# Layer border of a two-layer trunk: rows of x loaded in another place, sums and results tied differently, and the gate blocks of layer two run by token halves

## The chip, the cores and the metric

The kernel runs on one core of a Trainium2 chip. The core has a matrix engine (TensorE, PE in the profile), a vector engine (VectorE, DVE), a scalar engine (ScalarE, ACT), GpSimd (POOL) and SyncE (SP), whose queue issues most of the transfers. Each engine runs its instructions in the order in which they stand on it, and waits on semaphores for the others. The metric is the device time of one execution in microseconds, the median of several runs; less is better.

## The reference

Two layers of a hybrid trunk, on 512 tokens of width 2048, all in float32. Each layer normalises x, multiplies it by one wide input projection, runs two groups of heads on the columns, multiplies by an output projection, normalises again and adds the result to x:

```python
def hybrid_layer(x, w_in, w_out, g_pre, g_post, w_alpha, b_alpha, g_gla, g_att, rel_bias):
    h = rmsnorm(x, g_pre)
    z = h @ w_in
    gq, gk, gv, gg, ga, aq, ak, av, ag = split_columns(z)
    log_a = jax.nn.log_sigmoid(ga @ w_alpha + b_alpha) / GLA_TAU
    o_gla = rmsnorm(gla_chunk_causal(gq, gk, gv, log_a), g_gla) * jax.nn.silu(gg)
    o_att = rmsnorm(chunk_band_attention(aq, ak, av, rel_bias), g_att) * jax.nn.silu(ag)
    y = jnp.concatenate([o_gla, o_att], axis=-1) @ w_out
    return x + rmsnorm(y, g_post)

def reference(x, ...):
    h = x
    for l in range(DEPTH):          # DEPTH = 2
        h = hybrid_layer(h, ...)
    return h
```

(Shapes of heads are left out.) The border between the layers is what this document is about: the last output projection of layer one, `x + rmsnorm(y, g_post)`, the next layer's `rmsnorm(x, g_pre)`, and the next layer's first column blocks, the attention gate `ag`.

## The kernel before

**Weights.** Float32 products are made of three products of halves: each 1024-column piece of a weight block is split into a high part `wh` (cast on ACT, line 198) and a low part `wl` (difference on DVE, line 207), and each operand into a high and a low part in the same way (`split`: ACT line 105, DVE line 106). One weight *job* is 512 KB of weights: SP loads it into a ring (`raw`, five buffers, or `H`, four), ACT casts it (four buffers of `wh`), DVE makes the low part (three of `wl`), and PE runs twelve matmuls of 128x512 (line 387 in `fast_gemm`, 309 in `std_gemm`). `stream` is the list of all jobs of the program in the order of use, and `ahead` prepares loads, casts and low parts a few jobs ahead.

**A layer.** Two gate blocks AG0 and AG1 go through `std_gemm`, then six pairs of blocks through `fast_gemm`, which makes two block columns out of seven products P1 to P7 instead of eight, on sums and differences of the halves of weights and operands. Four jobs make one product. The output projection is two such pairs, W01 and W23; their products run P1, P2, P5, P6, P3, P7, P4. P7 subtracts two weight halves on DVE (line 194) and P4 adds two (line 192) before their casts. The operands of P5, P6, P3 and P7 come from DRAM (`sa<-oS`), one 512 KB load for each job; P4's lie in SBUF.

**The border.** The four token tiles are two halves. The products of W23 give results for one column block `j` and one token half `h` at a time, which are handed to `project`, which squares them for the norm (ACT line 1322) and multiplies by the gain (DVE lines 344 and 1326). When half 0 of the tokens is complete (after P3's result `(1, 0)`), `finish` runs for it: `finish_both` reduces the squares (DVE line 1365), takes the reciprocal root on GpSimd (`rsqrt`, line 429, a `pow`), and updates x, `z = y * r + z` (DVE line 1377), storing the result (GpSimd line 1380). `prep_half` squares the new rows (ACT line 442, reduce on DVE line 443), takes a second reciprocal root, scales the rows (DVE line 496), transposes them on PE (line 510), copies them out of PSUM with the gain (ACT line 521) and splits them into operands. When P4 is complete, the same runs for half 1, whose rows lie in narrower pieces (two of 1024 and four of 512). Its operands are read by the second half of the gate blocks, and the forget gate's weights are loaded behind it (`load_forget_gate`, lines 693 to 709).

The old x comes from DRAM row piece by row piece (`residual`, line 457), tied to certain jobs of W23.

**Order.** The source says little of when something runs. A scheduler puts the instructions of each engine into one order, by its own estimate of when each is ready and by the order of the source; `tc.issue_after(i)` only says that what follows must not stand ahead of `i`. In the source, work at the border is a list of generators (`tasks`), of which `pace` takes steps between the matmuls at a rate given for each product.

**Gate blocks of layer two.** AG0 runs for token half 0 (eight jobs), then again, with its weights loaded again, for half 1 (eight jobs); AG1 runs once for all four token tiles (eight jobs of 24 matmuls).

## Time and profile before

| | us |
|---|---|
| median of 3 runs (lowest, highest) | 1625.25 (1624.55, 1625.42) |
| profiled execution | 1624.26 |
| its span | 1622.5 |
| PE busy in the span | 1603.1 |
| DVE busy | 1263.3 |
| ACT busy | 909.8 |

The clock of PE was 0.998 of full in the profiled execution. W23's last products end near 809 us of the span, the gate blocks of layer two run from 810 to 913. In rows of the timeline the columns are start and duration in us, engine, line, operation, what it writes and reads, its shape, and in brackets the idle time of that engine just before it and what ended that; `xN` means N instructions drawn together. Tile names stand without their numbers: `sa` an operand from DRAM, `wh` and `wl` the parts of a weight block, `mm` and `ax` PSUM tiles, `g` any of the large slots in SBUF, `sm` small columns. The row of a window gives busy time of each engine in that stretch.

### The profile page before, as it was taken

The page shows a single profiled execution, that of the slowest core. Times are in us where ns is not written, and L with a number is a line of the kernel's source. Part 1 is how long each engine was busy: PE and PEld are TensorE (multiplying, and loading weights), DVE is VectorE, ACT ScalarE, POOL GpSimd, SP SyncE. Part 2 cuts the span into 40 slices and gives each one's busy share as a digit, 9 for nine tenths or more (in the row PEclk, how much of TensorE's full clock was granted, in tenths as well). Part 3 has the DMA queues.
Part 4 walks back from the last instruction along what each step waited for, and adds up shares of the span by engine and source line. Part 5 has one row for each costly group of instructions (what it writes and reads, how often), then busy time and mean ns, then how long its engine had stood idle before and what let it go on. Part 6 is the DMA issues. An engine that isn't in the chain of part 4 may idle for free.

```text
span 1622.5 us, 24443 instructions
## 1 busy us (share of the span) xinstructions
PE 1603.1 (99%) x8938; PEld 1372.6 (85%) x8938; DVE 1263.3 (78%) x1640; ACT 909.8 (56%) x1497; POOL 133.0 (8%) x192
## 2 busy tenths in 40 slices
PE   9999999999999999999999999999999999999997
PEld 7888999998888778878778889999988887788886
DVE  5977778678777868988987567686786778689887
ACT  7554445666554556655694444456575555466644
POOL 0120000000000010100222000000100000101001
PEclk9999999999999999999999999999999999999999
DMA  9797686785868768697879576867868687686887
GB/s 371 258 366 282 226 304 203 241 292 176 293 206 292 255 223 307 227 344 250 330 254 391 200 269 242 295 210 234 313 214 278 214 292 254 223 303 237 333 301 197
DMA packets 132777, 433.97 MB, mean 267 GB/s; under 512 B 14277, under 2 KB 27077, under 8 KB 132625
## 3 DMA queue, kind: packets, MB, share of 16 engines
q1 hardware_dynamic: 115920, 371.79, 65.9%
q0 software_dynamic: 16160, 59.53, 10.0%
q8 instruction: 71, 1.16, 0.3%
q10 hardware_dynamic: 576, 1.08, 0.2%
q14 instruction: 50, 0.40, 0.1%
HBM read 372.83 MB, written 61.62 MB: 268 GB/s over the span
## 4 chain that ended last, share of the span: by engine, by line
PE 93%; DVE 2%; DMA 2%; issue 1%; ACT 1%; POOL 0%; DVEq 0%; SPq 0%; ACTq 0%
PE mm L387 52%; PE mm L377 18%; PE mm L309 10%; PE ax L931 2%; PE ax L387 2%; PE ax L1117 1%; PE ax L914 1%; DVE wl L207 1%; PE ax L741 1%; DMA raw<-in_w_dram 1%; PE ax L1089 1%; PE ax L894 1%; PE ax L893 1%; PE ax L892 1%; DMA sa<-oS 1%
## 5 line engine op out<-in xcount | busy, mean ns | idle before, releaser
L387 PE MATMUL mm<-wh,sa 128*128 128x512 f32 x1600 | 517.8, 394 | 1.4 <-DMA sa<-oS 0.8
L207 DVE TENSOR_TENSOR wl<-H,wh 128x1024 fp32r<-128x1024 f32 x256 | 312.5, 1222 | 105.8 <-PE mm L387 33.6
L198 ACT CAST wh<-H 128x1024 fp32r<-128x1024 f32 x256 | 268.4, 1051 | 218.1 <-PE mm L387 92.6
L387 PEld LDWEIGHTS mm<-wh,sa 128*128 128x128 f32 x1600 | 299.5, 188 | 73.8 <-issue 9.7
L198 ACT CAST wh<-raw 128x1024 fp32r<-128x1024 f32 (+1 forms) x229 | 240.0, 1052 | 208.1 <-PE mm L387 96.6
L207 DVE TENSOR_TENSOR wl<-raw,wh 128x1024 fp32r<-128x1024 f32 (+1 forms) x229 | 278.0, 1218 | 63.9 <-PE mm L387 29.8
L387 PE MATMUL mm<-wl,sa 128*128 128x512 f32 x800 | 312.6, 391 | 0.0
L377 PE MATMUL mm<-sa,wh 128*128 128x256 f32 x1280 | 237.4, 285 | 0.0
L387 PE MATMUL mm<-wh,a 128*128 128x512 f32 x640 | 211.3, 394 | 1.5 <-ACT wh L198 1.5
L377 PEld LDWEIGHTS mm<-sa,wh 128*128 128x128 f32 x1280 | 200.2, 191 | 0.3
L377 PE MATMUL mm<-sa,wl 128*128 128x256 f32 x640 | 181.0, 283 | 0.2 <-DVE wl L207 0.2
L192 DVE TENSOR_TENSOR H<-H,raw 128x1024 f32<-128x1024 f32 x144 | 175.3, 1222 | 1.2
L387 PEld LDWEIGHTS mm<-wl,sa 128*128 128x128 f32 x800 | 150.3, 188 | 30.0 <-DVE wl L207 0.3
L387 PEld LDWEIGHTS mm<-wh,a 128*128 128x128 f32 x640 | 119.4, 188 | 26.7 <-ACT wh L198 1.9
L387 PE MATMUL mm<-wl,a 128*128 128x512 f32 x320 | 125.6, 393 | 0.0
L377 PEld LDWEIGHTS mm<-sa,wl 128*128 128x128 f32 x640 | 122.5, 191 | 0.4 <-DVE wl L207 0.4
L429 POOL TENSOR_TENSOR sm<-sm,mhalf 128x2 f32<-128x2 f32 (+2 forms) x40 | 57.3, 1433 | 761.2 <-DVE sm L941 457.0
L194 DVE TENSOR_TENSOR raw<-H,raw 128x1024 f32<-128x1024 f32 x60 | 73.4, 1224 | 49.9 <-DMA raw<-in_w_dram 49.5
L387 PE MATMUL mm<-wh,g 128*128 128x512 f32 x320 | 101.4, 390 | 0.6 <-ACT ev L339 0.6
L377 PE MATMUL mm<-a,wh 128*128 128x256 f32 x512 | 95.4, 285 | 0.0
L339 ACT COPY ev<-mm 128x512 f32<-128x512 f32 x104 | 60.8, 584 | 60.4 <-PE mm L387 44.0
L213 DVE TENSOR_TENSOR H<-H,raw 128x1024 f32<-128x1024 f32 x48 | 58.7, 1223 | 39.8 <-DMA raw<-in_w_dram 39.5
(246 smaller groups left out, 2313.5 us busy)
## 6 DMA issues: line engine op xcount, KB each, us to landing
raw<-in_w_dram SPq DMA_DIRECT2D x307, 512.0 KB, 5.1
sa<-S SPq DMA_DIRECT2D x184, 512.0 KB, 4.4
H<-in_w_dram SPq DMA_DIRECT2D x64, 512.0 KB, 5.4
sa<-A SPq DMA_DIRECT2D x48, 512.0 KB, 6.0
S<-g POOLq DMA_DIRECT2D x32, 512.0 KB, 9.0
sa<-oS SPq DMA_DIRECT2D x32, 512.0 KB, 4.8
oS<-g POOLq DMA_DIRECT2D x16, 512.0 KB, 4.5
oS<-sa POOLq DMA_DIRECT2D x16, 512.0 KB, 5.6
```

The costliest lines, as they stand in the source:

```text
L192: nc.vector.tensor_tensor(out=h, in0=h, in1=r, op=ALU.add)
L194: nc.vector.tensor_tensor(out=r, in0=h, in1=r, op=ALU.subtract)
L198: last_cast[0] = nc.scalar.copy(self.wh[:, z, :], src[:, z, :]).ins
L207: last_low[0] = nc.vector.tensor_tensor(out=self.wl[:, z, :], in0=self.src[:, z, :], in1=self.wh[:, z, :].bitcast(F32), op=ALU.subtract).ins
L213: nc.vector.tensor_tensor(out=h, in0=h, in1=self.src, op=ALU.add)
L309: nc.tensor.matmul(pss[o], a(part, kk, o) if callable(a) else a[:, part, t], rhs[:, kk, :], start=(i == 0 and kk == 0 and m == 0), stop=(i ...
L339: nc.scalar.copy(e, src[t])
L377: nc.tensor.matmul(dst, lhs[:, kk, f], a[:, part, tok], start=(fresh and kk == 0 and m == 0 and ft % 2 == 0), stop=(c == 3 and kk == 1 and ...
L387: last_mm[0] = nc.tensor.matmul(out_ps[t], a[:, part, tok], rhs[:, kk, :], start=(fresh and kk == 0 and m == 0), stop=(c == 3 and kk == 1 ...
L429: nc.gpsimd.tensor_tensor(out=out_r, in0=v, in1=mhalf[:, : v.shape[-1]], op=ALU.pow)
L741: nc.tensor.matmul(ps[0:96, half * 256 : (half + 1) * 256], wga[kt // 10][:, kt % 10, :], op[:, i, (kt % 2) * 256 : (kt % 2 + 1) * 256], s ...
L931: nc.tensor.matmul(o, self.pt[i][:, j * P : (j + 1) * P], av[hd // 4, j // 2][:, j % 2, (hd % 4) * P : (hd % 4 + 1) * P], start=(j == 0), ...
```

## The change

1. The rows of x for half 0 are loaded in W23's P1 and P2 behind jobs 2 and 3 of each instead of 0 and 1, those for half 1 in P5 and P6 instead of P6 and P7.
2. P4's weight sums of layer one's W23 are tied behind updates of x for half 0: the first behind the second update, the other three behind the fourth.
3. In W23 of layer one, the results of P7 (`(1, 1)`) are tied behind the last row scaling of half 0; the results `(1, 0)` and `(0, 0)`, of P3 and P2, lose their tie.
4. Of the four row scalings of half 0, the two of the first token tile run on ACT.
5. The gate blocks of layer two run AG0 and AG1 for half 0, then AG0 and AG1 for half 1: 32 jobs of twelve matmuls where there were sixteen of twelve and eight of 24. PE's matmuls are the same in number; eight more weight blocks are loaded, cast and split.

```diff
@@ Job.high
-                with tc.issue_after(lows[-2]) if self.b0 >= NB_IN else nullcontext():
+                with ExitStack() as ties:
+                    if self.b0 >= NB_IN:
+                        ties.enter_context(tc.issue_after(lows[-2]))
+                    if k == "P4" and self.l < L - 1 and self.b0 == W23[0]:
+                        ties.enter_context(tc.issue_after(half_adds[3 if self.c else 1]))
                     if k in ("P5", "P6") or (k == "P4" and self.b0 >= NB_IN):
                         nc.vector.tensor_tensor(out=h, in0=h, in1=r, op=ALU.add)
@@ stream
-            stream += [Job(l, "std", c, AG0) for c in CO]
-            stream += [Job(l, "std", c, AG0) for c in CO]
-            stream += [Job(l, "std", c, AG1) for c in CO]
+            stream += [Job(l, "std", c, b) for half in range(2) for b in (AG0, AG1) for c in CO]
@@ prep_half
-                last_row = nc.vector.tensor_scalar(
-                    out=xn[j][i], in0=z, scalar1=r[:, j : j + 1], scalar2=None, op0=ALU.mult
-                ).ins
+                if half == 0 and j == 0:
+                    nc.scalar.activation(xn[j][i], z, AF.Copy, scale=r[:, j : j + 1])
+                else:
+                    last_row = nc.vector.tensor_scalar(
+                        out=xn[j][i], in0=z, scalar1=r[:, j : j + 1], scalar2=None, op0=ALU.mult
+                    ).ins
@@ layer
-            std_gemm(l, AG0, (0, 1), CO, operand_in, gate_evac(0), rate=1.2)
-            tasks.append(token_sums(l))
-            tasks.append(forget_gate())
-            std_gemm(l, AG0, (2, 3), CO, operand_in, gate_evac(0), rate=0.8)
-            std_gemm(l, AG1, range(NT), CO, operand_in, gate_evac(1), rate=1.3, lag=2)
+            for half in range(2):
+                for q, b in enumerate((AG0, AG1)):
+                    std_gemm(
+                        l, b, (2 * half, 2 * half + 1), CO, operand_in, gate_evac(q), rate=1.3, lag=2 * half * q,
+                    )
+                if half == 0:
+                    tasks.append(token_sums(l))
+                    tasks.append(forget_gate())
@@ finish_both
-                        nc.vector.scalar_tensor_tensor(
-                            out=z, in0=yt, scalar=r[:, j : j + 1], in1=z, op0=ALU.mult, op1=ALU.add
+                        half_adds.append(
+                            nc.vector.scalar_tensor_tensor(
+                                out=z, in0=yt, scalar=r[:, j : j + 1], in1=z, op0=ALU.mult, op1=ALU.add
+                            ).ins
                         )
@@ out_consume
-                with nullcontext() if n and (j, h) == (0, 1) else tc.issue_after(last_low[0]):
+                if n and not last:
+                    behind = half_rows[0] if (j, h) == (1, 1) else None
+                else:
+                    behind = None if n and (j, h) == (0, 1) else last_low[0]
+                with tc.issue_after(behind) if behind else nullcontext():
                     project(o, n + j, src, gains[j] if n else None, comb, begin if ending else None)
@@ residual
-            elif k in ("P6", "P7") or (k in ("P1", "P2") and c < 2):
-                half = int(k in ("P6", "P7"))
+            elif k in ("P5", "P6") or (k in ("P1", "P2") and c >= 2):
+                half = int(k in ("P5", "P6"))
```

The lines of the changed kernel stand a few numbers further down: 207 is 211, 198 is 202, 192 is 196, 1326 is 1334, 1365 is 1373, 1377 is 1386, 443 is 445, 496 is 501 on DVE and 499 on ACT.

What that does to the order on DVE where P7 turns into P4, from the second reduce of half 0's squares on. Before, the low parts of P4's first three jobs (`wl<-H`) stand between and right behind the updates of x (L1377, written to `g_1405` to `g_1408`):

```order
L1365 TENSOR_REDUCE sm_7751<-ssy_6933 128x1
L207 TENSOR_TENSOR wl_7805<-H_7189,wh_7775 128x1024
L192 TENSOR_TENSOR H_7277<-H_7277,raw_7810 128x1024
L1377 SCALAR_TENSOR_TENSOR g_1405_7311<-a_1326_6929,sm_7752,g_1405_7311 128x1024
L1377 SCALAR_TENSOR_TENSOR g_1406_7312<-g_1439_7473,sm_7752,g_1406_7312 128x1024
L1377 SCALAR_TENSOR_TENSOR g_1407_7313<-a_1329_6935,sm_7752,g_1407_7313 128x1024
L1377 SCALAR_TENSOR_TENSOR g_1408_7314<-g_1442_7479,sm_7752,g_1408_7314 128x1024
L207 TENSOR_TENSOR wl_7841<-H_7241,wh_7808 128x1024
L192 TENSOR_TENSOR H_7335<-H_7335,raw_7846 128x1024
L207 TENSOR_TENSOR wl_7892<-H_7277,wh_7844 128x1024
L443 TENSOR_REDUCE sm_7784<-sm_7786 128x1
```

Now the same stretch reads:

```order
L1373 TENSOR_REDUCE sm_7753<-ssy_6933 128x1
L1386 SCALAR_TENSOR_TENSOR g_1421_7395<-a_1326_6929,sm_7754,g_1421_7395 128x1024
L1386 SCALAR_TENSOR_TENSOR g_1422_7396<-g_1439_7472,sm_7754,g_1422_7396 128x1024
L196 TENSOR_TENSOR H_7189<-H_7189,raw_7741 128x1024
L1386 SCALAR_TENSOR_TENSOR g_1423_7397<-a_1329_6935,sm_7754,g_1423_7397 128x1024
L1386 SCALAR_TENSOR_TENSOR g_1424_7398<-g_1442_7478,sm_7754,g_1424_7398 128x1024
L196 TENSOR_TENSOR H_7241<-H_7241,raw_7779 128x1024
L445 TENSOR_REDUCE sm_7785<-sm_7787 128x1
L211 TENSOR_TENSOR wl_7806<-H_7189,wh_7777 128x1024
L196 TENSOR_TENSOR H_7277<-H_7277,raw_7811 128x1024
L445 TENSOR_REDUCE sm_7785<-sm_7813 128x1
L211 TENSOR_TENSOR wl_7841<-H_7241,wh_7809 128x1024
```

The updates moved ahead of P4's first weight sum and low part, and directly behind the reduce.

On DVE during the first AG0 pass, from the second reduce of half 1's squares on (`wl_8065` is the low part of the fourth job, `wl_8087` of the fifth, `a_15...` are operands of half 0, `g_1457`, `sg` and `bias` the rows of half 1). Before:

```order
L1365 TENSOR_REDUCE sm_8054<-ssy_7201 128x1
L207 TENSOR_TENSOR wl_8065<-raw_8019,wh_8035 128x1024
L1377 SCALAR_TENSOR_TENSOR g_1457_7548<-g_1377_7197,sm_8055,g_1457_7548 128x1024
L1377 SCALAR_TENSOR_TENSOR g_1458_7549<-g_1538_7903,sm_8055,g_1458_7549 128x1024
L207 TENSOR_TENSOR wl_8087<-raw_8037,wh_8067 128x1024
L106 TENSOR_TENSOR a_1548_7933<-H_7930,a_1548_7933 128x512
L1377 SCALAR_TENSOR_TENSOR sg_7550<-g_1380_7203,sm_8055,sg_7550 128x512
L1377 SCALAR_TENSOR_TENSOR sg_7551<-g_1380_7203,sm_8055,sg_7551 128x512
L106 TENSOR_TENSOR a_1550_7943<-H_7930,a_1550_7943 128x512
```

Now:

```order
L211 TENSOR_TENSOR wl_8065<-raw_8019,wh_8035 128x1024
L1334 TENSOR_TENSOR g_1541_7909<-mm_7292,t_1396_7285 128x512
L1373 TENSOR_REDUCE sm_8054<-ssy_7201 128x1
L106 TENSOR_TENSOR a_1548_7933<-H_7930,a_1548_7933 128x512
L106 TENSOR_TENSOR a_1550_7943<-H_7930,a_1550_7943 128x512
L106 TENSOR_TENSOR a_1556_7972<-H_7969,a_1556_7972 128x512
L1386 SCALAR_TENSOR_TENSOR g_1449_7506<-g_1377_7197,sm_8055,g_1449_7506 128x1024
L1386 SCALAR_TENSOR_TENSOR g_1450_7507<-g_1538_7903,sm_8055,g_1450_7507 128x1024
L1386 SCALAR_TENSOR_TENSOR sg_7508<-g_1380_7203,sm_8055,sg_7508 128x512
L1386 SCALAR_TENSOR_TENSOR sg_7509<-g_1380_7203,sm_8055,sg_7509 128x512
L1386 SCALAR_TENSOR_TENSOR bias_7510<-g_1541_7909,sm_8055,bias_7510 128x512
L1386 SCALAR_TENSOR_TENSOR bias_7511<-g_1541_7909,sm_8055,bias_7511 128x512
```

Here the fifth job's low part, which stood behind two updates, stands right behind all six.

On ACT behind P4's casts, `g_1518` and `g_1519` being the scaled rows of the first token tile, `H_7853` the first operand out of PSUM. Now:

```order
L202 CAST wh_7844<-H_7277 128x1024
L499 ACTIVATE g_1518_7821<-g_1421_7395,sm_7786 128x1024
L499 ACTIVATE g_1519_7823<-g_1422_7396,sm_7786 128x1024
L202 CAST wh_7895<-H_7330 128x1024
L202 CAST wh_7960<-raw_7897 128x1024
L1330 ACTIVATE t_1540_7906,ssy_7195<-t_1539_7904 128x512
L202 CAST wh_7999<-raw_7962 128x1024
L526 ACTIVATE H_7853<-ax_7848,gcol 128x256 x2
```

Before, the two L499 were not on this engine.

More of the change, by code (lines that the diff above doesn't have):

```diff
@@ L482, in hybrid_trunk @@
     full = {}
-    half_lows, half_turns, half_rows = [], [], [None]
+    half_adds, half_lows, half_turns, half_rows = [], [], [], [None]
     def prep_half(l, half, xs):
```

## The prediction

> **What bounds the kernel now.** I read the page's first and fourth parts, then the idle rows of TensorE (PE) in the timeline around the layer border, then the engines that end those waits.
>
> ```profile
> PE 1603.1 (99%) x8938; PEld 1372.6 (85%) x8938; DVE 1263.3 (78%) x1640; ACT 909.8 (56%) x1497; POOL 133.0 (8%) x192
> PE 93%; DVE 2%; DMA 2%; issue 1%; ACT 1%; POOL 0%; DVEq 0%; SPq 0%; ACTq 0%
> ```
>
> PE is the bound: 1603.1 of a 1622.5 us span, and both kernels give it the same matmuls. Only bubbles can move. Those within reach of the change:
>
> ```profile
> 771.00 0.84 PE L387 MATMUL mm<-wh,sa 128*128 128x512 f32 x3
> 771.68 0.39 PE L387 MATMUL mm<-wl,sa 128*128 128x512 f32 x1
> ...
> 785.98 0.39 PE L387 MATMUL mm<-wh,sa 128*128 128x512 f32 x1
> 786.61 0.47 PE L387 MATMUL mm<-wh,sa 128*128 128x512 f32 x1 [0.23 <-DMA sa<-oS]
> ...
> 789.22 0.39 PE L387 MATMUL mm<-wh,sa 128*128 128x512 f32 x1
> 790.18 0.47 PE L387 MATMUL mm<-wh,sa 128*128 128x512 f32 x1 [0.58 <-DMA sa<-oS]
> ...
> 792.80 0.39 PE L387 MATMUL mm<-wh,sa 128*128 128x512 f32 x1
> 793.83 0.50 PE L387 MATMUL mm<-wh,g 128*128 128x512 f32 x1 [0.64 <-ACT ev L339]
> ...
> 801.92 0.39 PE L387 MATMUL mm<-wh,g 128*128 128x512 f32 x1
> 803.60 0.33 PE L510 MATMUL ax<-cst,g 128*128 128x128 f32 x1 [1.29 <-DVE g L496]
> ...
> 822.16 0.61 PE L309 MATMUL mm<-wl,a 128*128 128x512 f32 x2
> ...
> 824.20 0.84 PE L309 MATMUL mm<-wh,a 128*128 128x512 f32 x3
> 825.19 0.50 PE L309 MATMUL mm<-wl,a 128*128 128x512 f32 x1
> 835.58 0.33 PE L510 MATMUL ax<-cst,g 128*128 128x128 f32 x1 [0.61 <-ACT g L521]
> 838.61 0.33 PE L510 MATMUL ax<-cst,g 128*128 128x128 f32 x1 [0.92 <-ACT g L521]
> 839.46 0.50 PE L309 MATMUL mm<-wh,g 128*128 128x512 f32 x1 [0.19 <-ACT g L105]
> ```
>
> Matmuls of 512 columns start 0.227 us apart (771.00, three of them, 771.68), so a weight block's twelve take 2.72 us. Start to start against that pace, the gaps cost more than the bracket shows: 786.61 costs 0.40, 790.18 costs 0.73 (both P7, waiting for operands), 793.83 costs 0.80 (P7 to P4), the half-0 transposes 1.45 and about 0.5, 825.19 costs 0.31 (three starts from 824.20 would be 824.88), the half-1 transposes up to 839.46 about 2.6 (with two small waits between). That is some 7 us, 0.43% of the time: the most the change can give.
>
> **The change part by part.** An operation on VectorE (DVE) or ScalarE (ACT) overlaps the next by some 0.08 us, so its pace is its duration less that: the first two starts below (784.93, 786.07) are 1.14 apart at 1.22 each.
>
> ```profile
> 779.22 1.22 DVE L194 TENSOR_TENSOR raw<-H,raw 128x1024 f32<-128x1024 f32 x1
> 784.93 1.22 DVE L207 TENSOR_TENSOR wl<-raw,wh 128x1024 fp32r<-128x1024 f32 x1
> 786.07 1.22 DVE L192 TENSOR_TENSOR H<-H,raw 128x1024 f32<-128x1024 f32 x1
> ...
> 787.80 0.15 DVE L1365 TENSOR_REDUCE sm<-ssy 128x1 f32<-128x5 f32 x1
> ...
> 792.04 1.28 DVE L1377 SCALAR_TENSOR_TENSOR g<-g,sm,g 128x1024 f32<-128x1024 f32 x1
> ...
> 802.79 2.74 DVE L496 TENSOR_SCALAR g<-g,sm 128x1024 f32<-128x1024 f32 x4 [0.61 <-POOL sm L429]
> ...
> 820.06 1.41 DVE L1377 SCALAR_TENSOR_TENSOR sg<-g,sm,sg 128x512 f32<-128x512 f32 x2
> ```
>
> Columns: start, duration, engine, line, operation. So: a low part (wl) or a weight sum 1.14, a reduce 0.06, a residual update 1.20 (half width 0.66), a row scaling 0.66; a half-width product 0.60 (row 801.49 further down).
>
> *Rows of x.* Six half-1 loads and the fourth half-0 load leave P7's stretch, where DMA stood at 408 GB/s (row 780 to 800 below). P7 then needs one operand and one weight block, 1.05 MB per 2.72 us, 385 GB/s: I take its two waits, 1.13 us, as gone, and P7's end at 791.9. In P5/P6 a job now brings an operand and at most a row, again 385 GB/s, with operands issued four jobs ahead: I take nothing. Bounds: 0 and the same 1.13 back.
>
> *P4's sums and P7's results.* DVE now goes: reduce, four updates with two of P4's sums among them, and only then P4's low parts. From 780.36 (779.22 + 1.14): half-width 0.60, wl 1.14, half-width twice, the first reduce, P7's last wl 1.14, half-width, the second reduce: 4 x 0.60 + 2 x 1.14 + 0.12 + 0.1 (duration of the last) = 785.25. Then the rsqrt on GpSimd:
>
> ```profile
> 540.48 0.71 POOL L429 TENSOR_TENSOR sm<-sm,mhalf 128x2 f32<-128x2 f32 x1 [41.00 <-DVE sm L433]
> 788.11 2.69 POOL L429 TENSOR_TENSOR sm<-sm,mhalf 128x2 f32<-128x2 f32 x1 [2.92 <-DVE sm L1365]
> 799.93 2.82 POOL L429 TENSOR_TENSOR sm<-sm,mhalf 128x2 f32<-128x2 f32 x1 [3.39 <-DVE sm L443]
> 801.49 0.69 DVE L344 TENSOR_TENSOR t<-ev,ev 128x512 f32<-128x512 f32 x1
> ```
>
> The same 128x2 op takes 0.71 us with DVE idle and 2.7 to 2.8 when DVE runs two-input operations back to back: the one at 799.93 ends 0.57 after DVE's last (801.49 + 0.69). In the new order DVE has nothing between the second reduce and the update, so I take 0.71, with 0.25 from reduce to rsqrt (787.80 + 0.15 to 788.11, and the hand-over): first update at 786.24. With 2.69 it is 788.2; that end goes into the range. [...]
>
> Then 2 x 1.20 + 1.14 + 2 x 1.20 + 1.14 + 0.06 (reduce) + 1.14 (wl of P4's first job) + 1.14 + 0.06 = 9.5: second reduce done at 795.7. P4's first wl is ready at 794.6, where PE wants it 0.45 after 791.9: a new wait of about 2.25 us in P4's first job. So what the three removed waits gave (1.13 + 0.80) is spent here. Behind that wl nothing else of P4 is late: its second job's wl is done at 796.9. The second rsqrt has two DVE operations behind it and ends 0.57 after them, so row scaling starts at 798.7 (before: 802.79). The transposes then wait about 0.2 instead of 2; the gate starts near 809.3.
>
> *Row scaling on ACT.* Two scalings leave DVE (1.3 us), two come to ACT, about 0.96 each. There they stand ahead of everything that makes the gate's operands:
>
> ```profile
> 805.50 2.30 ACT L521 ACTIVATE H<-ax,gcol 128x256 f32<-128x256 f32 x6 [1.45 <-PE ax L510]
> ...
> 812.48 0.66 ACT L1322 ACTIVATE t<-mm 128x512 bf16<-128x512 f32 x1
> ...
> 815.91 1.17 ACT L198 CAST wh<-raw 128x1024 fp32r<-128x1024 f32 x1
> 816.85 1.79 ACT L105 CAST a<-H 128x512 fp32r<-128x512 f32 x3
> ```
>
> Pace: L521 0.36, L105 0.52, L1322 0.60 with its accumulator read, a cast 0.95 (815.91 to 816.85). From 798.7 ACT runs without a pause: 2 scalings, 5 casts, 16 of L521, 4 of L105 and one like it, 4 squares of L1322: 1.9 + 4.8 + 5.8 + 2.6 + 2.4 = 17.5, so the last square that half 1's residual needs is done at 816.2 (before: 812.48 + 0.66 = 813.1). DVE then: low part, product, reduce, three operand low parts (L106, 0.60 each) and, 0.57 after these, the third rsqrt: half 1's first update at 819.9 (before 815.93).
>
> *Half 1's updates.* All six now stand in one piece ahead of the low part of AG0's fifth block: 2 x 1.20 + 4 x 0.66 = 5.0, then 1.14: wl at 826.1. PE reaches that wl at 809.3 + 4 x 2.72 + 0.45 = 820.7 and waits 5.4 us. Before, it passed the same matmul at 822.16.
>
> *Gate blocks by halves.* Half 1's transposes now have two AG1 jobs between them and 16 us until their operands are read, so no operand of half 1 is late if its rows are in time. After the wl at 826.1 DVE has an operand's low part, three wl, two reduces, six small low parts of the forget gate's weights (the row below), the fourth rsqrt (0.6 behind the last of these) and six scalings: 0.6 + 3.4 + 0.1 + 1.4 + 0.6 + at most 4.0 = 836.2, against PE's need at 826.1 + 2.3 + 3 x 2.72 + 0.45 = 837.0. The 2.6 us at 835 to 839 go, and the 0.3 at 825. Price: eight more blocks, each 512 KB of DMA, a cast (0.95) and a low part (1.14): 7.6 us on ACT and 9.1 on DVE, covered by the idle time in the windows below (columns: window, length, busy PE, PEld, DVE, ACT, POOL, clock, DMA share, GB/s).
>
> ```profile
> L106 DVE TENSOR_TENSOR g<-t,g 128x160 fp32r<-128x160 f32 (+1 forms) x6 | 1.4, 288 | 2.6 <-ACT g L105 2.6
> ```
>
> ```profile
> 780.00:800.00 20.00, 18.55 (x80) 14.33 (x79) 19.04 (x24) 12.88 (x21) 5.22 (x10) 1.00 1.03 408
> ...
> 865.00:888.00 23.00, 23.00 (x117) 19.46 (x116) 14.26 (x19) 10.09 (x15) 6.41 (x12) 1.00 1.03 408
> ...
> 900.00:913.00 13.00, 13.00 (x59) 10.78 (x58) 4.10 (x4) 4.02 (x6) 1.66 (x3) 1.00 0.55 197
> ```
>
> DVE is busy 14.26 of 23 us from 865 and 4.10 of the last 13, ACT less, so I cost these at nothing; without that room it would be the 9.1 us of DVE. DMA has none until 900: 4.2 MB more at 408 GB/s is 10 us of transfers, which find room after 900, if PE's lead of weights lasts that long. I take 0; the other end is the first rival. On SP's queue the load of the forget gate's w_ga now follows AG1's first block; that block's buffer is free when the fourth AG0 block's low part is done (817), and a load takes 4 to 5 us, so it is there before the 827 at which ACT wants it. GpSimd's stores of the updated rows go out with the updates, 0.54 us each, and nothing of the chain is queued behind them but the next rsqrt, which comes later anyway.
>
> **Sum.** PE passes the marked matmul 826.1 - 822.2 = 3.9 us (4.0 with the restart) later; the waits after it that go are 2.9. Net +1.1 us: profiled 1624.26 becomes 1625.4; the median of the runs shown is 1.0 above the profiled run, so 1626.4. Own range: -1 (second rsqrt not held up, 2 us) to +3.2 (first rsqrt 2.69, or P5/P6 paying the 1.13).
>
> **Rivals.** *Slower: weight loads starve in the second half of the gate.* Blocks are used every 2.72 us (193 GB/s) where AG1's took 5.44. Five raw buffers and 2.1 us of cast and low part hold that pace only while a load lands within 5 x 2.72 - 2.1 = 11.5 us.
>
> ```profile
> raw<-in_w_dram SPq DMA_DIRECT2D x4, 512.0 KB, 7.0
> ...
> q1 hardware_dynamic: 1382, 1.90, 31.8%
> ...
> raw<-in_w_dram SPq DMA_DIRECT2D x2, 512.0 KB, 13.7
> ```
>
> The DMA view has 7.0 us in 858 to 870 (first row), but 13.7 in 876 to 892, while the sum stores (q0) run beside it. There SP's queue moved 1.90 MB in 16 us, 119 GB/s; at that rate the blocks fall 16 x (1 - 119/193) = 6.1 us behind, less the one or two blocks of lead. Against it: part of that queue's trouble then was two small-packet loads, now issued later. Time: 1.1 + 3.4 to 6.1, about 1631. [...]
>
> *Faster: the fifth block's low part is in time.* If half 1's square is done 5 us earlier than I add up, the 5.4 us wait does not form; what stays is 2.25 + 0.2 against some 7 of now: -4.5, 1620.8. For it: my sum stacks seventeen us of ACT pieces, any idle of which would be visible only now. Against: each pace is measured in this very stage.
>
> *It does nothing:* rows still collide with P7's operands. Then P4's wait is shorter by as much, since it hangs on DVE; no change of the sum.
>
> **How the numbers follow.** Likeliest, within 0.2% (3.25 us, about what a measurement of this kernel tells from no change): 0.44. Starved loads: 0.31. Low part in time: 0.25. So faster 0.25, same 0.44, slower 0.31; the range 1620.5 to 1631.5 takes in both rivals' times and leaves some 0.1 on each side.
>
> **What would show it.** Right: no wait for sa in P7; a wait of about 2 us for wl in P4's first job; the fifth AG0 job waiting some 5 us for wl behind six updates; nothing at half 1's transposes. Wrong: the first rsqrt near 2.7, that wl in time, or PE waiting for wl or wh with raw landings over 11.5 us between 850 and 915.

## The result and the profile after

The changed kernel takes 1629.8 us (median of 11 runs, 1627.23 to 1631.46) where the kernel before, on the same chip, takes 1625.47 (11 runs, 1623.95 to 1629.13): ratio 1.0023, 95% interval [1.0014, 1.0032]. On a second chip it was 1629.39 against 1625.06, 1.0024 [1.0014, 1.0033]. The forecast was 1626.4, with a time within 0.2% of the kernel before as the likeliest outcome. The time lies inside the range of 1620.5 to 1631.5, but on its slow side, and just beyond what was called no change: a small loss of some 4 us.

The profiled execution took 1630.47 us, its span 1628.4. From the page of the changed kernel, busy times and the chain that ended last:

```profile
PE 1605.2 (99%) x8938; PEld 1374.1 (84%) x8938; DVE 1271.8 (78%) x1646; ACT 919.2 (56%) x1507; POOL 128.9 (8%) x192
PE 89%; DVE 3%; DMA 3%; issue 2%; ACT 1%; POOL 0%; DVEq 0%; SPq 0%; POOLq 0%; ACTq 0%
```

PE runs the same 8938 matmuls and is busy 2.1 us longer, so some of them must have been slower. In the chain PE's share falls from 93% to 89%; DVE, DMA and issue take a point more each.

The two traces have to be laid over each other first. The first fence is PE's timeline after, at the start of W23, the second the same matmul before:

```profile
728.30 0.73 PE L389 MATMUL mm<-wh,a 128*128 128x512 f32 x2 [1.52 <-ACT wh L202]
```

```profile
725.72 0.73 PE L387 MATMUL mm<-wh,a 128*128 128x512 f32 x2 [1.52 <-ACT wh L198]
```

The profiled run stands 2.58 us later here, mostly from operand and weight waits at 110 to 156 us, in layer one, where both kernels have the same instructions: PE idles 0.79 us in 100 to 130 and 0.87 in 130 to 160 after, and not at all in either stretch before. Times below that are compared with the kernel before have these 2.58 us taken off.

PE's timeline after, from P7's end on:

```profile
795.29 0.51 PE L389 MATMUL mm<-wh,g 128*128 128x512 f32 x1 [0.22 <-ACT ev L341]
796.82 0.50 PE L389 MATMUL mm<-wh,g 128*128 128x512 f32 x1 [1.02 <-ACT ev L341]
798.38 0.50 PE L389 MATMUL mm<-wl,g 128*128 128x512 f32 x1 [1.06 <-DVE wl L211]
...
829.51 0.79 PE L311 MATMUL mm<-wl,a 128*128 128x512 f32 x1 [5.12 <-DVE wl L211]
830.10 1.05 PE L311 MATMUL mm<-wh,a 128*128 128x512 f32 x2
830.96 0.63 PE L311 MATMUL mm<-wl,a 128*128 128x512 f32 x1
831.38 0.63 PE L311 MATMUL mm<-wh,a 128*128 128x512 f32 x1
```

Three things stand here. P4's first job waits three times, 3.0 us in all against the pace of 0.227. The fifth AG0 block waits for its low part: 5.28 us start to start beyond the pace. And behind that wait the matmuls start 0.427 us apart (830.96, 831.38) instead of 0.227; up to 834.8 this loses 2.56 us (5.28 us for twelve matmuls, which take 2.72 at the pace). Nothing waits at half 1's transposes.

The windows say why (length, then busy time of PE, PEld, DVE, ACT and POOL, then PE's granted clock, DMA share, GB/s):

```profile
823.00:829.50 6.50, 1.40 (x7) 0.82 (x5) 6.50 (x9) 6.50 (x13) 3.30 (x7) 0.88 0.66 251
829.50:832.00 2.50, 2.49 (x6) 2.01 (x7) 2.50 (x3) 2.19 (x10) 0.00 (x0) 0.50 1.32 287
832.00:835.00 3.00, 3.00 (x9) 2.31 (x8) 2.74 (x10) 0.82 (x1) 1.53 (x1) 0.54 0.73 270
835.00:838.00 3.00, 3.00 (x14) 2.44 (x13) 3.00 (x8) 0.94 (x2) 0.00 (x0) 1.00 0.98 380
```

The granted clock is 0.50 and 0.54 for five us behind the idle time, then 1.00. This idle time of PE is paid twice: once as the wait, 5.28 us, and once more at half clock, 2.56.

DVE's timeline, up to that low part:

```profile
788.93 0.15 DVE L1373 TENSOR_REDUCE sm<-ssy 128x1 f32<-128x5 f32 x1
789.98 1.29 DVE L1386 SCALAR_TENSOR_TENSOR g<-a,sm,g 128x1024 f32<-128x1024 f32 x1 [0.90 <-POOL sm L431]
...
797.10 1.22 DVE L211 TENSOR_TENSOR wl<-H,wh 128x1024 fp32r<-128x1024 f32 x1
...
823.20 2.47 DVE L1386 SCALAR_TENSOR_TENSOR g<-g,sm,g 128x1024 f32<-128x1024 f32 x2
825.59 1.41 DVE L1386 SCALAR_TENSOR_TENSOR sg<-g,sm,sg 128x512 f32<-128x512 f32 x2
826.91 1.41 DVE L1386 SCALAR_TENSOR_TENSOR bias<-g,sm,bias 128x512 f32<-128x512 f32 x2
828.24 1.22 DVE L211 TENSOR_TENSOR wl<-raw,wh 128x1024 fp32r<-128x1024 f32 x1
```

The six updates of half 1 run without a pause, the low part behind them, and PE starts as it ends (829.46, 829.51).

### The profile page after: what moved, and what is told of

It is laid out like the page before. It is cut to its first block, busy times and chain, and to the rows that moved or that the text cites. A ratio compares the mean times of both kernels' runs of the same rounds, so it can differ in the third digit from the quotient of the medians.

```text
span 1628.4 us, 24480 instructions
## 1 busy us (share of the span) xinstructions
PE 1605.2 (99%) x8938; PEld 1374.1 (84%) x8938; DVE 1271.8 (78%) x1646; ACT 919.2 (56%) x1507; POOL 128.9 (8%) x192
## 4 chain that ended last, share of the span: by engine, by line
PE 89%; DVE 3%; DMA 3%; issue 2%; ACT 1%; POOL 0%; DVEq 0%; SPq 0%; POOLq 0%; ACTq 0%
PE mm L389 49%; PE mm L379 20%; PE mm L311 8%; PE ax L939 2%; PE ax L389 2%; DMA raw<-in_w_dram 1%; PE ax L1125 1%; PE ax L922 1%; DVE wl L211 1%; PE ax L1097 1%; PE ax L902 1%; PE ax L901 1%; PE ax L900 1%; DMA H<-in_w_dram 1%; DMA S<-g 1%
## 5 line engine op out<-in xcount | busy, mean ns | idle before, releaser
L202 ACT CAST wh<-raw 128x1024 fp32r<-128x1024 f32 (+1 forms) x237 | 248.5, 1052 | 200.9 <-PE mm L389 90.4
L211 DVE TENSOR_TENSOR wl<-raw,wh 128x1024 fp32r<-128x1024 f32 (+1 forms) x237 | 287.6, 1216 | 68.1 <-PE mm L389 27.1
L431 POOL TENSOR_TENSOR sm<-sm,mhalf 128x2 f32<-128x2 f32 (+2 forms) x40 | 53.0, 1324 | 762.5 <-DVE sm L949 459.2
```

What stands on the lines that cost most here:

```text
L202: last_cast[0] = nc.scalar.copy(self.wh[:, z, :], src[:, z, :]).ins
L211: last_low[0] = nc.vector.tensor_tensor(out=self.wl[:, z, :], in0=self.src[:, z, :], in1=self.wh[:, z, :].bitcast(F32), op=ALU.subtract).ins
L431: nc.gpsimd.tensor_tensor(out=out_r, in0=v, in1=mhalf[:, : v.shape[-1]], op=ALU.pow)
```

## The experiments

To compare traces without the noise of other layers, each gets one number: the time from PE's 4251st matmul (in W23, 758.08 in the kernel before) to its 5001st (behind the gate blocks, 922.16), called the stretch: 164.08 us before (in e5 and e10, which have 20 matmuls more in it, to the 5021st). It is given as a difference to that, one profiled execution each; the ratio comes from five rounds of runs beside the kernel before.

| kernel | ratio to before, 95% | stretch |
|---|---|---|
| changed | 1.0023 [1.0014, 1.0032] | +3.84 |
| changed, again (e9) | 1.0024 [1.0014, 1.0033] | +3.80 |
| e1: fifth low part between the updates | 1.0006 [0.9998, 1.0015] | +0.14 |
| e2: without part 5 | 1.0018 [1.0009, 1.0027] | +3.13 |
| e3: part 5 alone | 0.9981 [0.9972, 0.9989] | -1.41 |
| e4: e1, and P4's first sum untied | 0.9982 [0.9973, 0.9990] | -3.36 |
| e5, e10: 20 more matmuls in the wait | 1.0018 [1.0009, 1.0027], 1.0012 [1.0003, 1.0020] | +1.83, +1.77 |
| e6: without part 2 | 0.9972 [0.9961, 0.9982] | -4.28 |
| e7: without part 4 | 1.0003 [0.9993, 1.0013] | -0.07 |
| e11: part 2 alone | 0.9978 [0.9968, 0.9988] | -2.50 |
| e12: without parts 2 and 4 | 0.9982 [0.9972, 0.9992] | -2.34 |

**e1: the fifth block's low part between the updates of half 1.** In the changed kernel's `finish_both`:

```diff
-                    with tc.issue_after(half_lows[3 + n // 2]) if pair else nullcontext():
+                    with ExitStack() as ties:
+                        if pair:
+                            ties.enter_context(tc.issue_after(half_lows[3 + n // 2]))
+                            if n >= 2:
+                                ties.enter_context(tc.issue_after(last_low[0]))
                         half_adds.append(
```

> The changed kernel with one tie more: the third of half 1's six updates stands behind the newest low part, so the low part of AG0's fifth block stands between the second and the third update instead of behind all six; nothing else on VectorE changes place. Theory (the long wait costs itself and then a slow clock): the fifth block's wait falls from 5.1 us idle to about 2.5, and the matmuls behind it keep 0.227 us where they took 0.427 for 4.9 us of the changed kernel's profile; gain over the changed kernel 2.65 + 2.4 = 5 us, near 1624.8, level with the kernel before. If the clock falls after a short wait too, the gain is 2.65 us or less. Rival (the eight more weight blocks and their transfers cost the time): gain under 1 us.

Measured: 1626.14 us against 1625.97. The timeline of the kernel, DVE and PE:

```profile
820.40 2.48 DVE L1390 SCALAR_TENSOR_TENSOR g<-g,sm,g 128x1024 f32<-128x1024 f32 x2
...
822.79 1.22 DVE L211 TENSOR_TENSOR wl<-raw,wh 128x1024 fp32r<-128x1024 f32 x1
...
824.07 0.50 PE L311 MATMUL mm<-wl,a 128*128 128x512 f32 x1 [2.47 <-DVE wl L211]
```

The low part stands behind two updates instead of six, and the wait of 5.28 us is 2.63. Some six matmuls behind it still start 0.427 us apart (1.15 us lost), and the sixth block then waits 0.73. The time is level with the kernel before, as expected, but the clock falls behind the shorter wait too, and the stretch is 3.7 us shorter than the changed kernel's, not 5. So the place of one 1.14 us instruction on DVE is worth as much as the whole loss.

**e2 and e3: part 5 (the gate by halves) undone, and alone.** In `layer` and in `stream`, e2 takes the changed kernel and e3 the kernel before, with

```diff
-            for half in range(2):
-                for q, b in enumerate((AG0, AG1)):
-                    std_gemm(
-                        l, b, (2 * half, 2 * half + 1), CO, operand_in, gate_evac(q), rate=1.3, lag=2 * half * q,
-                    )
-                if half == 0:
-                    tasks.append(token_sums(l))
-                    tasks.append(forget_gate())
+            std_gemm(l, AG0, (0, 1), CO, operand_in, gate_evac(0), rate=1.2)
+            tasks.append(token_sums(l))
+            tasks.append(forget_gate())
+            std_gemm(l, AG0, (2, 3), CO, operand_in, gate_evac(0), rate=0.8)
+            std_gemm(l, AG1, range(NT), CO, operand_in, gate_evac(1), rate=1.3, lag=2)
```

and the three old lines of `stream` in e2, and the reverse of both in e3.

> The changed kernel with the gate blocks run as before (part five undone), the other four parts kept; VectorE's order up to AG0's fifth block stays that of the change. Theory: the 5.1 us wait and the slow clock behind it stay, since they hang on the updates; the half-1 transposes wait again for ScalarE, some 2 us: 1630 to 1632, no faster than the changed kernel. Rival (gate blocks by halves are what costs): 1625 to 1627.

> The kernel before with the gate blocks by halves alone (part five). Theory: the waits of half 1's transposes at 835 to 839 (2.6 us) go and nothing comes in their place: 2 to 3 us faster than before, near 1622.7. Rival (eight more weight blocks starve the transfers): 1 us slower or more.

Measured: e2 1628.88, e3 1622.6, each against 1625.97. In e2 the wait at the fifth block stays (5.26 us) and so do the slow matmuls behind it, but half 1's transposes do not wait although AG0 runs twice again. So the waits that part 5 was to remove at 835 to 839 are not tied to it: they are in the profile before (and in e8, which has its border) and in no other. Part 5 alone is a gain of 3.4 us in the median; its profiled execution, the longest of the twelve runs, has -1.4 in the stretch, with 1.6 us lost to a slow clock at half 0's transposes. Beside the other parts no gain of part 5 is seen: the intervals of e2 and of the changed kernel overlap.

**e4: e1, and P4's first weight sum free.** The tie of e1 stands here on all six updates; on DVE the low part comes behind two of them, as in e1.

```diff
-                    if k == "P4" and self.l < L - 1 and self.b0 == W23[0]:
-                        ties.enter_context(tc.issue_after(half_adds[3 if self.c else 1]))
+                    if k == "P4" and self.c and self.l < L - 1 and self.b0 == W23[0]:
+                        ties.enter_context(tc.issue_after(half_adds[3]))
...
+                            if n >= 0:
+                                ties.enter_context(tc.issue_after(last_low[0]))
```

> The changed kernel with the tie of the first experiment, and P4's first weight sum no longer tied behind the updates of half 0 (the other three behind the fourth update). Theory: beside the 5 us of the first experiment the wait of P4's first job (3.0 us) falls to about 1.4: near 1623, 0.1 to 0.2% faster than before. Rival (half 0's updates come 1.9 us later, and the chain to the gate with them): no faster than the first experiment.

Measured: 1622.34 against 1625.97. P4's first low part now stands ahead of half 0's updates; in the trace P4 still waits 1.23 us for a copy on ACT, 0.51 and 0.69 in its second job, and the sixth AG0 block 0.48. No matmul is slow. With the low part between the updates as in e1, freeing one sum is worth another 3.5 us.

**e5 and e10: the wait filled with work.** The fifth block's first matmuls by the high part are followed by twenty more, into a PSUM tile that nothing reads:

```diff
+                    if (l, blk, o, i, kk, m) == (1, AG0, 0, 4, 0, 1):
+                        idle = ps_mm.tile([P, W], F32, tag="mm", name=nm("mm"))
+                        for _ in range(20):
+                            nc.tensor.matmul(idle, a[:, 0, t], job.wh[:, 0, :], start=True, stop=True)
                     nc.tensor.matmul(
```

> The changed kernel with twenty more matmuls of 128x512 on PE, between the fifth AG0 block's first matmuls by the high part and those by its low part, written into a PSUM tile that nothing reads. Theory A (the idle time itself halves the clock): the twenty take 20 x 0.227 = 4.5 us of the 5.1 us wait, the matmuls behind it start 0.227 us apart instead of 0.427, and the kernel with more work is 2.4 us faster than the changed one: 1627.4, ratio to the kernel before 1.0009. Theory B (the 0.427 spacing comes from what runs beside it there, the updates and stores of half 1 or late weight parts): the spacing stays and the time is the changed kernel's 1629.8 or later, ratio 1.0023 or more.

> The changed kernel as it is, beside the next three on one chip. Its ratio to the kernel before was 1.0023 [1.0014, 1.0032]: 1629 to 1630 here, and in the trace the wait of 5.1 to 5.3 us at the fifth AG0 block with some 2 us lost to matmuls 0.427 us apart behind it.

> The kernel with twenty more matmuls in that wait, beside the changed one on one chip, since 1.0018 [1.0009, 1.0027] against 1.0023 [1.0014, 1.0032] told nothing apart. Theory A (the idle time halves the clock, and the slow matmuls are on the path): 2 us less than the changed kernel. Theory B (what the clock costs there is had back further on): the same as the changed kernel within 0.5 us, though no matmul is slow.

Measured: e5 1628.39 against 1625.04; e9 and e10, on one chip, 1629.39 and 1627.08 against 1625.06. PE's timeline of e10, and a window of it:

```profile
823.32 4.70 PE L314 MATMUL mm<-wh,a 128*128 128x512 f32 x20
...
828.83 0.50 PE L315 MATMUL mm<-wl,a 128*128 128x512 f32 x1 [0.59 <-DVE wl L211]
829.17 0.64 PE L315 MATMUL mm<-wh,a 128*128 128x512 f32 x2
829.65 0.40 PE L315 MATMUL mm<-wl,a 128*128 128x512 f32 x1
```

```profile
828.80:832.00 3.20, 3.17 (x14) 2.60 (x15) 3.20 (x7) 2.75 (x11) 0.14 (x1) 1.00 1.02 246
```

DVE has the same updates, stores and low parts beside them, the matmuls start 0.227 apart (829.17, two of them, 829.65), the clock is 1.00, and the stretch is 2.0 us shorter in both profiles, with 20 matmuls more in it. The medians of e9 and e10 differ by 2.3 us, but their intervals overlap, so the size rests on the traces. Theory A stands: behind 5.12 us of idle time the clock was 0.50, behind 0.59, with the same work on DVE beside it, 1.00.

The trace of e9 shows another form of it, PE's timeline and its clock in P4:

```profile
796.04 0.49 PE L389 MATMUL mm<-wh,g 128*128 128x512 f32 x1 [1.02 <-ACT ev L341]
797.60 0.63 PE L389 MATMUL mm<-wl,g 128*128 128x512 f32 x1 [1.07 <-DVE wl L211]
798.03 1.05 PE L389 MATMUL mm<-wh,g 128*128 128x512 f32 x2
```

```profile
797.50:801.50 4.00, 3.90 (x10) 3.08 (x11) 3.52 (x5) 1.51 (x2) 2.67 (x1) 0.57 1.01 366
```

Here the same two short waits that left the clock alone in the first profile of this kernel halve it, 1.6 us lost. The fifth block's wait is then 4.04 us instead of 5.28, and the stretch as long as the first time (+3.80, +3.84): PE comes later to a low part whose time DVE sets.

**e6: part 2 undone.** P4's sums stand where the scheduler puts them:

```diff
-                    if k == "P4" and self.l < L - 1 and self.b0 == W23[0]:
-                        ties.enter_context(tc.issue_after(half_adds[3 if self.c else 1]))
```

> The changed kernel without part 2: P4's weight sums stand where the scheduler puts them. Theory A (part 2 is what makes the rest late): the first P4 job's wait of 3.0 us goes back to about 1, the fifth AG0 block's low part stands behind two updates of half 1 instead of six, PE waits there at most 1 us and its clock stays; 6 to 8 us less than the changed kernel: 1622 to 1624, ratio 0.998 to 0.999. Rival (part 4, the two scalings on ACT, makes half 1's updates late): the wait at the fifth block stays above 3 us with its slow clock, and the time above 1626.

Measured: 1620.23 against 1625.04, the fastest kernel of all here, ahead of both. DVE's timeline:

```profile
816.14 2.48 DVE L1384 SCALAR_TENSOR_TENSOR g<-g,sm,g 128x1024 f32<-128x1024 f32 x2
818.54 1.22 DVE L209 TENSOR_TENSOR wl<-raw,wh 128x1024 fp32r<-128x1024 f32 x1
```

Half 1's updates start 7.1 us ahead of the changed kernel's 823.20, 4.8 with the runs laid over each other (758.45 against 760.68 at the stretch's start), and the fifth low part stands behind two of them: PE does not wait there, nor does its clock fall. ACT's timelines show why the updates come sooner: half 1's last two squares (`t<-mm`, line 1328) start at 810.48 and 812.52 behind eight of the sixteen copies of half 0 out of PSUM, in the changed kernel (line 1330) at 817.13 and 819.35 behind fourteen and sixteen; laid over each other, the last square is 4.6 us earlier. P4 waits 1.19 and 0.85 us. Beside the other four parts, part 2 costs 8 us by the stretch.

**e7: part 4 undone.** All four row scalings on DVE:

```diff
-                if half == 0 and j == 0:
-                    nc.scalar.activation(xn[j][i], z, AF.Copy, scale=r[:, j : j + 1])
-                else:
-                    last_row = nc.vector.tensor_scalar(
-                        out=xn[j][i], in0=z, scalar1=r[:, j : j + 1], scalar2=None, op0=ALU.mult
-                    ).ins
+                last_row = nc.vector.tensor_scalar(
+                    out=xn[j][i], in0=z, scalar1=r[:, j : j + 1], scalar2=None, op0=ALU.mult
+                ).ins
```

> The changed kernel without part 4: all four row scalings on DVE. The scheduler then puts the fifth AG0 block's low part ahead of the six updates of half 1, and the sixth block's behind them. Theory A (part 2 makes the rest late, part 4 little): P4's wait of 3 us stays, the half-0 transposes wait 1.3 us more, the wait moves from the fifth block to the sixth and is some 3 us instead of 5, with a slow clock behind it: 1627 to 1629. Rival (ACT's chain, 1.9 us shorter here, makes half 1's updates late): the wait falls under 1.5 us, the clock stays, 1624 to 1625.5.

Measured: 1624.23 against 1625.04. The time is the rival's, the trace is not. DVE's timeline, then PE's:

```profile
824.67 1.22 DVE L211 TENSOR_TENSOR wl<-raw,wh 128x1024 fp32r<-128x1024 f32 x1
825.80 2.47 DVE L1383 SCALAR_TENSOR_TENSOR g<-g,sm,g 128x1024 f32<-128x1024 f32 x2
```

```profile
832.12 0.73 PE L311 MATMUL mm<-wh,a 128*128 128x512 f32 x2 [0.73 <-ACT wh L202]
833.32 0.50 PE L311 MATMUL mm<-wl,a 128*128 128x512 f32 x1 [0.47 <-DVE wl L211]
```

Against the start of the stretch (762.90 here, 760.68 in the changed kernel) the updates begin 0.4 us later than in the changed kernel, not earlier. Whether ACT's shorter chain hastens them is not shown: the low part, 1.14 us, now stands ahead of them, and this profile lost 1.7 us at half clock behind P4's waits. What is gone is the long wait, since the low part stands ahead of the updates. Without that half clock PE would have come sooner to the two waits left, 1.5 us, which would then be near theory A's 3 us; but no slow clock followed them, and the half-0 transposes did not wait, which theory A had wrong. The profiled execution, 1629.32 us, is 5 us above the median of this kernel's runs.

**e11 and e12: part 2 alone, and parts 2 and 4 both undone.** e11 is the kernel before with the tie of part 2, e12 the changed kernel with the edits of e6 and e7.

```diff
+                    if k == "P4" and self.l < L - 1 and self.b0 == W23[0]:
+                        ties.enter_context(tc.issue_after(half_adds[3 if self.c else 1]))
```

> The kernel before with part 2 alone: P4's weight sums tied behind the updates of half 0, DVE in the order of the changed kernel there. Theory A (part 2 is the loss, whatever else is changed): a wait of 3 us in P4's first job, half 1's updates late, so that a wait at the fifth or sixth AG0 block is added, and half 1's transposes wait at least as long as before: 1628 to 1632, ratio 1.002 to 1.004. Rival (part 2 costs only beside part 4): the P4 wait is paid, less what the transposes of half 0 had waited, 1625 to 1626.5.

> The changed kernel without parts 2 and 4. Theory A (part 4 costs only through the order that the scheduler then chooses, and nothing once part 2 is gone): the same as without part 2 alone, 1620.2, within 1 us. Rival (part 4 is a loss by itself): 1 to 3 us less than that, 1617 to 1619. Other rival (part 4 is a gain by itself, since the transposes of half 0 have their rows 1.3 us sooner): 1 to 2 us more, 1621 to 1622.

Measured: e11 1622.87 and e12 1621.77, each against 1625.06. Theory A of e11 is wrong, and so is its rival: part 2 alone is a gain of 2.2 us. PE's timeline of e11, P7's operands to the sixth AG0 block:

```profile
786.49 0.47 PE L391 MATMUL mm<-wh,sa 128*128 128x512 f32 x1 [0.21 <-DMA sa<-oS]
789.73 0.47 PE L391 MATMUL mm<-wh,sa 128*128 128x512 f32 x1 [0.24 <-DMA sa<-oS]
793.01 0.47 PE L391 MATMUL mm<-wh,sa 128*128 128x512 f32 x1 [0.32 <-ACT t L446]
797.44 0.50 PE L391 MATMUL mm<-wh,g 128*128 128x512 f32 x1 [1.02 <-ACT ev L343]
...
828.33 0.50 PE L313 MATMUL mm<-wl,a 128*128 128x512 f32 x1 [1.83 <-DVE wl L211]
```

P7 loses 1.25 us to its waits, so P4 comes later and waits 1.3 instead of 3.0; half 0's transposes, which waited some 2 us before, do not wait; half 1's transposes do not wait; and the fifth block's low part stands ahead of the updates, so only the sixth waits, 1.99 us. As for e12, undoing part 4 as well does not help: 1621.77 against e6's 1620.23, -2.34 against -4.28 in the stretch. Those medians come from two chips and their ratios' intervals overlap, so that part 4 is a gain of 1.5 to 1.9 us beside parts 1, 3 and 5 is likely and not shown. Of the three expectations the last fits best; that part 4 is a loss by itself has the data against it.

**e8: the clock by itself.** In the kernel before, the low part of the second P3 job is made 5 to 10 times over in six pairs of layer one, so that PE waits for different lengths:

```diff
+    LATE = {
+        (0, AV0, "P3", 1): 4, (0, QK01, "P3", 1): 5, (0, QK45, "P3", 1): 6,
+        (0, GK, "P3", 1): 7, (0, GV0, "P3", 1): 8, (0, GG0, "P3", 1): 9,
+    }
...
-                    last_low[0] = nc.vector.tensor_tensor(
...
+                    for _ in range(1 + LATE.get((self.l, self.b0, self.kind, self.c), 0)):
+                        last_low[0] = nc.vector.tensor_tensor(
```

> The kernel before, in which the low part of the second P3 job is made 5, 6, 7, 8, 9 and 10 times over in six pairs of layer one, so that PE waits there for the last of them, each time some 1.1 us longer. Theory A (the clock drops in proportion to the idle time, from the shortest ones on): matmuls 0.427 us apart behind each wait of over 1 us, some 0.4 to 0.5 us lost for each us of idle (2.36 behind 5.1 and about 1.1 behind 2.5 so far). Theory B (there is a threshold near 3 us, and behind it one fixed loss): no slow matmuls behind the waits under it, the same 2 to 2.5 us behind all above.

Measured: 1657.88 us, one run; the waits are what counts. PE's timeline, then the windows behind three of them:

```profile
143.40 0.99 PE L394 MATMUL mm<-wh,sa 128*128 128x512 f32 x2 [2.05 <-DMA sa<-S]
...
428.49 0.50 PE L394 MATMUL mm<-wl,sa 128*128 128x512 f32 x1 [2.26 <-DVE wl L213]
...
528.33 1.19 PE L394 MATMUL mm<-wh,sa 128*128 128x512 f32 x2 [4.81 <-DMA sa<-S]
...
636.40 1.19 PE L394 MATMUL mm<-wh,sa 128*128 128x512 f32 x2 [5.67 <-DMA sa<-S]
```

```profile
143.40:147.20 3.80, 3.80 (x10) 2.98 (x11) 2.35 (x2) 0.00 (x0) 0.00 (x0) 0.55 0.94 338
...
428.50:432.00 3.50, 3.50 (x18) 3.04 (x19) 3.50 (x5) 0.88 (x1) 0.00 (x0) 1.00 0.68 225
...
530.50:536.00 5.50, 5.50 (x13) 4.33 (x14) 3.51 (x3) 0.88 (x1) 0.00 (x0) 0.50 0.35 124
```

Both theories fall. After 2.05 us idle the clock is 0.55 for 3.8 us; after 2.26 us it is 1.00. So it is neither in proportion to the idle time nor a matter of a length of 3 us. What it is a matter of can be read from these traces; it stands in the last section.

## Why the prediction was right or wrong

**The bubbles within reach.** Right: what the change moves lies between 758 and 922 us of the span. Ahead of that the two traces differ by 2.6 us, most of it in layer one, and the later one makes up 0.5 behind it.

**Rows of x: P7's two waits, 1.13 us, gone, and nothing paid in P5/P6.** Half right. P7 waits for no operand, but other jobs of W23 do: 0.57 us in P3, just ahead of P7 (PE at 781.20), in the changed kernel, 0.46 and 0.75 in P6 in e9, 0.86 in e10, and none in e1. Where part 1 is not in (e3, e11), P7 has 1.1 to 1.25 us of waits. In most of these profiles the value lies nearer to the other end that the prediction kept, the same 1.13 back.

**The first rsqrt 0.71 us, the second held up.** Right, in GpSimd's timeline after:

```profile
789.23 0.71 POOL L431 TENSOR_TENSOR sm<-sm,mhalf 128x2 f32<-128x2 f32 x1 [1.79 <-DVE sm L1373]
...
799.61 2.76 POOL L431 TENSOR_TENSOR sm<-sm,mhalf 128x2 f32<-128x2 f32 x1 [2.80 <-DVE sm L445]
```

DVE was idle during the first (0.90 us, up to 789.98). The second ends at 802.37, again 0.57 behind DVE's last two-input operation (801.80).

**P4's first low part at 794.6, a wait of 2.25 us.** The mechanism held, the size was 3.0. The second reduce ended at 786.50 (788.93 + 0.15 - 2.58) where the sum had 785.25, and the low part was ready at 795.74 (797.10 + 1.22 - 2.58): DVE stood 1.1 us further back than added up. Why it did was not tried.

**ACT's chain, the last square at 816.2, half 1's first update at 819.9, the low part at 826.1, PE waits 5.4 us.** Close: the updates began at 820.62, the low part was there at 826.88, PE waited 5.28. The order of DVE and paces from the old trace gave the low part's time to within 0.8 us. That the wait came out to within 0.2 is luck in part: PE wanted the low part at 821.65 (829.51 - 5.28 - 2.58) where the sum had 820.7, so both ends came about as much late. And the pieces that the prediction lists for DVE ahead of the first update add to 4.2 us, which gives 820.4 and not 819.9.

**"PE passes the marked matmul 826.1 - 822.2 = 3.9 us (4.0 with the restart) later."** This is the step that failed. PE passed it 4.77 us later (829.51 - 2.58 - 822.16), and the restart, put at 0.1 us, cost 2.56: PE's clock is halved for some 5 us behind this wait, and e5 and e10 give 2.0 us of it back by keeping PE busy. With 4.77 and 2.56 in their places, and 2.9 still taken off, the predicted +1.1 is +4.4 and the stretch measures +3.84. The prediction bounded nothing here: the longest idle time in its rows of PE is 1.29 us, and it took the price of a restart behind short waits (0.11 us behind 825.19, in its profile before) for a wait four times as long.

**The waits that go after it, 2.9 us.** They went, and a little more: from the marked matmul to the end of the stretch it is 100.00 us before and 99.09 after, 2.56 of them for the slow matmuls, so 3.5 us went. That they belong to part 5 is not: e2 and e11, without part 5, do not have them either.

**Eight more blocks at nothing; the rival of starved loads.** From the DMA view of 885 to 915 us and the windows, both after:

```profile
raw<-in_w_dram SPq DMA_DIRECT2D x7, 512.0 KB, 12.3
```

```profile
888.00:913.00 25.00, 25.00 (x139) 21.55 (x138) 17.52 (x22) 12.41 (x17) 5.93 (x11) 1.00 1.03 414
```

The median of these seven loads is over the 11.5 us at which the rival was to decide, and yet PE is busy 25.00 of 25.00 us. Some loads over the mark are not enough, then; that the lead of weights absorbed them is likely and was not tried. The rival's time, 1631, lay nearer to the result than the forecast, but its cause is not there. The cost at nothing holds: part 5 alone is a gain.

**The range.** That the time lies inside it is luck. The sum's own ends, -1 and +3.2, give 1624.3 to 1628.5, and 1629.8 is outside them; the stated range takes it in only because it was drawn out to the time of the starved loads, which did not happen.

**The faster rival, the low part in time.** It did not happen, but its price was right in kind: e1 and e6, which bring it about by other means, take 3.7 and 8 us from the changed kernel.

What stays open is the sign of single parts. Part 2 is a gain of 2.2 us on the kernel before and a loss of 8 beside the others; the place of the fifth low part explains most of it (behind two updates or ahead of all six in e6, e7 and e11, behind all six in the changed kernel), not all, as e4 and e12 show. In e6 half 1's updates also start sooner, with ACT's squares ahead of half of the copies; why the scheduler chose that order was not tried.

## What to carry to other kernels

Price an idle time of the matrix engine twice: here 4 to 6 us of idle cost 1.6 to some 3 us more at half clock, so a wait filled with matmuls that nobody needs was cheaper than the idle one (e10), and two waits with work between them can go without the second price, as the changed kernel's 1.30 and 1.33 us in P4 did. After any change of ties or engines, look where the scheduler has put the next low part among the long vector work: one such instruction moved past four updates is worth the whole change. Gains of ties do not add up, so undo each part of a change that came out even: the best kernel here is the change without its part 2 (1620.23, ratio 0.9972).

## What the hardware showed

PE's granted clock is 1.00 or 0.50 in these traces (a figure between is the mean of a window that holds both), and at half clock matmuls of 512 columns start 0.427 us apart. Counted over all profiles: behind idle times of 4 us and more matmuls were slow in five of five cases (5.28, 5.26, 4.04, 4.98, 5.83 us, start to start beyond the pace). The wait of 1.68 us at the start of W23 is in all fourteen profiles; slow matmuls follow it in two (e7, e11). The pair of waits of 1.30 and 1.33 us in P4 is in seven, with slow matmuls in two (e7, e9). So short waits do it sometimes, with the same instructions around them.

Where they fall tells the two apart. In each of the fourteen traces the changes of the clock between the first matmuls and the last lie on one grid of 3.41 us, and half clock lasts one step of it (e1, e9), two (the changed kernel, 827.96 to 834.78, 6.82 us) or three (e8). How the grid lies against the program differs from run to run: half clock begins 1.55 us ahead of the matmul that ends the fifth block's wait in the changed kernel (829.51), and some 0.2 ahead of the same matmul in e9 (828.71; clock 0.98 over 824.00 to 828.70). Two windows are two steps of the grid, in e11 and then in the changed kernel, with the wait of 1.68 us in the first step of each:

```profile
724.27:727.68 3.41, 1.73 (x7) 0.80 (x5) 0.91 (x1) 3.05 (x6) 0.00 (x0) 1.00 1.03 410
727.68:731.10 3.42, 3.37 (x8) 2.69 (x9) 1.45 (x2) 1.80 (x5) 0.00 (x0) 0.50 1.03 410
```

```profile
725.56:728.97 3.41, 1.89 (x8) 0.97 (x6) 0.69 (x1) 2.83 (x5) 0.00 (x0) 1.00 1.04 413
728.97:732.38 3.41, 3.20 (x15) 2.60 (x15) 1.83 (x3) 2.55 (x6) 0.00 (x0) 1.00 1.03 410
```

The wait itself is 1.52 us of idle time. In e11 its step holds 0.16 us more, 1.68 in all, and the next step runs at half clock; in the changed kernel it holds no more, and the next runs at 1.00. Over all steps at full clock in the fourteen traces, the thirteen that half clock follows have 1.63 us or more of idle time; of all the others one has 1.65 (e11, 826.67) and the next 1.57. So in these traces half clock follows steps in which PE idled for about half of the 3.41 us. A step at half clock with 0.93 us or more of idle time was followed by another, one with 0.32 or less by full clock. This settles e8: the 2.26 us lay as 0.78 and 1.48 in two steps, the 2.05 us in one. The two waits in P4 lay in one step in e7 and e9 (2.26 and 2.20 us idle) and in two in the changed kernel (1.24 and 1.06). As an estimate from these counts, a wait of over 3.3 us, twice the 1.65, has more than 1.65 in one step however it falls and should halve the clock, as the five above did; one of under 1.6 us alone stays short of the 1.63.
